# Half rows of the modulation queued behind chosen additions on VectorE in a SwiGLU FFN

## The chip, the cores and the metric

The kernel runs on one core of a Trainium2 chip. The metric is the device time of one execution in microseconds (us), as the median of several runs.

## The reference

Two layers of a diffusion trunk run over 1280 tokens (256 context, 1024 latent) of width 1024, in float32. What matters here is the modulation, computed from the two conditioning vectors, and the FFN that it scales:

```python
def ada_modulation(cond, w, b):
    m = jax.nn.silu(cond) @ w + b
    return jnp.split(m[:, None, :], N_MOD, axis=-1)
...
        sh1, sc1, g1, sh2, sc2, g2 = ada_modulation(cond, w_ada[l], b_ada[l])
...
        h2 = rms_norm(x, norm2_g[l]) * (1.0 + sc2) + sh2
        gate, up = jnp.split(h2 @ w_ffn_in[l], 2, axis=-1)
        x = x + g2 * ((jax.nn.silu(gate) * up) @ w_ffn_out[l])
```

`m` has 6 x 1024 entries per layer and conditioning. The FFN has 2816 hidden features, 22 tiles of 128.

## The kernel before

**Matrix products.** A float32 matrix is split into two parts that TensorE multiplies at full rate: ScalarE casts the high part, VectorE subtracts it (`split`, line 107). Each product is three matmuls (`mm3`, `product`).

**FFN in.** For each of the 22 feature tiles, gate and up are computed for three chunks of tokens: the context (256) and two latent halves (512 each). The two latent halves use a scheme with seven products instead of eight per pair of 512-column blocks: sums of weight quarters are formed on GpSimd (`sums`, lines 156 to 169) and sums of activations once per layer (`act_sums`). A first loop over the features 0 to 6 does their context part and, for the features 1 to 5 (`PRE`), two of the seven products, kept in DRAM. Then `seven(f, ...)` (line 1287) does a whole feature, and `five(f)` (line 1324) the rest of a kept one, with its kept parts loaded (`kept`). The order is 6, then 7, 1, 8, 2, 9, 3, 10, 4, 11, 5, 12, 0, 13 to 21 (`AFTER`). Results go to DRAM (`keep_ft`).

In a seven, a PSUM tile is copied by ScalarE (`copied`) and the accumulation in it goes on; `V.tensor_add(u3, u3, pc)` (L1304) reads the tile `pc`, into which a later product accumulates; `V.tensor_mul(g1, g1, pa_)` (L1308) ends the first latent half, and the additions and multiplications at L1316 and L1318 the second. In a five, `V.tensor_add(u2, p1, pa_)` (L1330) adds the kept product to the first of the PSUM tiles, into which the third product then accumulates; L1334 and L1336 form u3.

**Modulation in the FFN.** A row tile j of the modulation is a dot product of 128 rows of the transposed weight with both conditioning vectors. `ada_half` (line 280) does half of its columns: a load of 128 x 512 into tile `ra` (two buffers), and for each of the two vectors one multiply-reduce on VectorE (L286) with the sum in `mod`; its full output goes to a PSUM tile that nothing reads. The vectors' halves lie in `condh`, one buffer, loaded anew when the half changes. `ada_halves(n)` takes the next n from a list: 16 are issued during the projection before the FFN in each layer, and 48 (layer 0) and 16 (layer 1) at points within `seven` and `five`.

**What sets the order.** TensorE's order is that of the program (`manual_schedule`). The other engines, in this part, are ordered by the tile scheduler, which puts an instruction where it expects it to be ready; each engine and SP's DMA queue then runs its instructions in that order. Weights are fetched ahead (`fetch`, `load_w`) into two `raw` buffers and one more (`rx`), and split into four buffers `w` and three `wh`.

Of the kernel before, what the change touches and what calls it, by code (L numbers as in the profile page):

```python
# [39 lines left out]
FIRST = 7  # L40
# [9 lines left out]
def build(tc, d):  # L50
    nc = tc.nc
    V, S, G, PE = nc.vector, nc.scalar, nc.gpsimd, nc.tensor
# [11 lines left out]
    def nm(s):  # L64
        uid[0] += 1
        return f"{s}_{uid[0]}"
# [138 lines left out]
    def load_w(n, ahead=4):  # L205
        fetch(ahead)
        return [ready.pop(0) for _ in range(n)]
# [72 lines left out]
    def ada_half(l, j, u, pool, first):  # L280
        wt = pool.tile([P, 512], F32, tag="ra", bufs=2, name=nm("ra"))
        nc.sync.dma_start(wt, d["w_adaT"][l, j, :, u * 512:(u + 1) * 512])
        junk = psum()
        for q in range(2):
            o = mods[l][:, j, q:q + 1]
            V.tensor_tensor_reduce(  # L286
                out=junk, in0=wt, in1=pools["condh"][:, q], scale=1.0,
                scalar=cols[:, C_ADA + l * 48 + j:C_ADA + l * 48 + j + 1] if first else o,
                op0=ALU.mult, op1=ALU.add, accum_out=o)
# [252 lines left out]
    for l in range(DEPTH):  # L542
# [420 lines left out]
        for j in range(NQ + 3):  # L963
            if j < NQ:
# [27 lines left out]
                if j > 2 and mix_ld:  # L992
                    c, y = mix_ld.pop(0)
                    t0, n = CH[c]
# [73 lines left out]
        def fpsum(n):  # L1068
            return fps.tile([P, 512], F32, tag="f", bufs=6, name=nm("f"))[:, :n]
# [28 lines left out]
        if l == 0:  # L1098
            late += [(1, j) for j in range(2 * KD)]
        halves = [(a, j, u, x == 0) for b in (early, late) for x, u in enumerate((0, 1) if b is early else (1, 0))  # L1100
                  for a, j in b]

        def ada_halves(n):
            for _ in range(min(n, len(halves))):
                a, j, u, first = halves.pop(0)
                if pools.get("u") != u:
                    pools["u"] = u
                    t = pools["condh"] = fpa.tile([P, 2, 512], F32, tag="ch", name=nm("condh"))
                    nc.sync.dma_start(t, CS[:, u * 512:(u + 1) * 512].partition_broadcast(P))
                ada_half(a, j, u, fpa, first)  # L1110
# [65 lines left out]
        def keep_ft(f, c, sg):  # L1176
            t0, n = CH[c]
            nc.gpsimd.dma_start(FS[l][f, :, t0:t0 + n], sg)  # L1178
# [4 lines left out]
        def copied(ps):  # L1183
            t = fpa.tile([P, 512], F32, tag="cp", bufs=3, name=nm("pc"))
            S.copy(t, ps)
            return t

        def ctx_gate(w):
            pg = fpsum(CH[0][1])
            proj(pg, w, h2[0])  # L1190
            return pg

        def ctx_up(w, f, pg):
            n = CH[0][1]
            pu = fpsum(n)
            if isinstance(w, tuple):
                w = quarter(w[0], 0) + w[1]
            else:
                w = [wslice(w, k) for k in range(KD)]
            mm3(pu, [w[k] + (h2[0][:, 0, k], h2[0][:, 1, k]) for k in range(KD)])  # L1200
            sg = gtile(n)
            S.activation(sg, pg, AF.Silu)
            V.tensor_mul(sg, sg, pu)
            keep_ft(f, 0, sg)
# [21 lines left out]
        def quarter(w, i):  # L1226
            return [wslice(w, 4 * i + j) for j in range(4)]
# [5 lines left out]
        def product(ps, a, b, first=True):  # L1233
            i = 0
            for (wh, wl), (xh, xl) in zip(a, b):
                for y, z in ((wl, xh), (wh, xl), (wh, xh)):
                    PE.matmul(ps, lhsT=y, rhs=z, start=(first and i == 0), stop=(i == 11),  # L1237
                              skip_group_check=not first)
                    i += 1
# [3 lines left out]
        def product1(wg):  # L1243
            ps = fpsum(512)
            product(ps, quarter(wg, 0), b11)
            return wg, ps, copied(ps)


        def product2(wg, p1):
            pb = fpsum(512)  # L1250
            product(pb, quarter(wg, 1), b21)
            g1 = gtile()
            V.tensor_add(g1, p1, pb)
            S.activation(g1, g1, AF.Silu)
            return g1
# [31 lines left out]
        def seven(f, wg, pa_, p1, s24, wh, rest, more, ctx, lead):  # L1287
            first = not callable(rest)
            if lead:
                g1 = product2(wg, p1)  # L1290
            product(pa_, quarter(s24, 0), t2, False)
            u2 = copied(pa_)
            if not lead:
                g1 = product2(wg, p1)
            if ctx:
                pg = ctx_gate(wg)
                ada_halves(int(f > FIRST))
            a21, s31 = (None, rest) if first else rest()
            pc = fpsum(512)
            product(pc, quarter(s31, 1), t1)  # L1300
            product(pa_, quarter(s31, 0), t3, False)
            u3 = copied(pa_)
            nxt = product1(load_w(1, 1)[0]) if more else None
            V.tensor_add(u3, u3, pc)  # L1304
            if ctx and not more:
                ctx_up((a21, wh), f, pg)
            product(pa_, wh, t4, False)
            V.tensor_mul(g1, g1, pa_)  # L1308
            keep_ft(f, 1, g1)
            ada_halves(int(f > FIRST))  # L1310
            if ctx and more:
                ctx_up((a21, wh), f, pg)
            fetch(1)
            product(pc, quarter(s24, 1), b22, False)
            g2 = gtile()
            V.tensor_add(g2, u2, pc)  # L1316
            S.activation(g2, g2, AF.Silu)
            V.tensor_mul(g2, g2, u3)  # L1318
            keep_ft(f, 2, g2)
            ada_halves(int(f != FIRST))  # L1320
            return nxt


        def five(f):
            s24, wh = load_w(1, 1)[0]
            p1, g1 = kept(f, 2, "cp"), kept(f, 1, "g")
            pa_, pc = fpsum(512), fpsum(512)
            product(pa_, quarter(s24, 0), t2)
            u2 = fpa.tile([P, 512], F32, tag="cp", bufs=3, name=nm("pc"))
            V.tensor_add(u2, p1, pa_)  # L1330
            s31 = load_w(1, 1)[0]
            product(pc, quarter(s31, 1), t1)
            u3 = fpa.tile([P, 512], F32, tag="cp", bufs=3, name=nm("pc"))
            V.tensor_add(u3, p1, pc)  # L1334
            product(pa_, quarter(s31, 0), t3, False)
            V.tensor_add(u3, u3, pa_)  # L1336
            ada_halves(int(f > 1))
            product(pc, quarter(s24, 1), b22, False)
            g2 = gtile()
            V.tensor_add(g2, u2, pc)  # L1340
            S.activation(g2, g2, AF.Silu)
            V.tensor_mul(g2, g2, u3)
            keep_ft(f, 2, g2)
            fetch(1)
            product(pa_, quarter(wh, 0), t4, False)
            V.tensor_add(p1, p1, pa_)
            V.tensor_mul(g1, g1, p1)
            keep_ft(f, 1, g1)
# [4 lines left out]
        for f, g in zip(AFTER, AFTER[1:] + (None,)):  # L1353
# [8 lines left out]
            def rest():  # L1362
                return load_w(2, 2)
# [8 lines left out]
        for c in range(3):  # L1372
            t0, n = CH[c]
            xs[c] = opened(xp, f"x{c}", side="right").tile([P, KD, n], F32, name=nm("x"))
        for k in range(KD):
            for c in range(3):
                t0, n = CH[c]
# [198 lines left out]
```

## Time and profile before

| | |
|---|---|
| median of 3 runs | 3073.92 us (3070.77 to 3078.88) |
| the profiled execution | 3073.52 us, span 3071.8 us |
| TensorE busy | 2925.8 us, 95% of the span |
| VectorE busy | 2012.9 us, 66% |
| ScalarE busy | 1109.5 us, 36% |
| GpSimd busy | 682.7 us, 22% |
| mean granted TensorE clock | 0.982 |

The profile is one execution. Busy time is an average over stages with different limits, so the stretch of the FFN is read by itself. Engines are called PE (TensorE), PEld (its weight loads), DVE (VectorE), ACT (ScalarE), POOL (GpSimd) and SP (the queue that issues most loads); L1304 is line 1304 of the kernel before. In a timeline, brackets give the idle time before an instruction and what ended it.

### The profile page before, as it was taken

What the parts mean: (1) busy time and instruction counts of PE and PEld (TensorE: products, weight loads), DVE (VectorE), ACT (ScalarE), POOL (GpSimd) and SP (SyncE); (2) the same over time, 40 slices, a digit from 0 to 9 for tenths busy, and PEclk for the clock granted to TensorE, in tenths of its full rate; (3) what the DMA queues carried; (4) which work ended last, traced back from release to release, by engine and by line L of the source; (5) the groups of instructions that cost most, each with busy time, mean ns of one, the idle gap of its engine ahead of it and who ended that gap; (6) DMA issues with size and microseconds to landing.
All of it is one profiled execution on the core that took longest, in us unless ns stands there. A gap on an engine that the chain in (4) does not pass through costs nothing.

```text
span 3071.8 us, 41522 instructions
## 1 busy us (share of the span) xinstructions
PE 2925.8 (95%) x15800; PEld 2504.0 (82%) x15800; DVE 2012.9 (66%) x3221; ACT 1109.5 (36%) x1887; POOL 682.7 (22%) x756
## 2 busy tenths in 40 slices
PE   7999899998899999999988998999989999999997
PEld 4888788886688888888877887888868888888886
DVE  6767787689864333777677677876874443347777
ACT  4423677163222332211252236761622223222112
POOL 1222200034343333000022222000444433310002
PEclk9999999999999999999999999999999999999998
DMA  6576633444432222512225665434442221152211
GB/s 225 159 219 189 175 93 87 164 139 134 154 117 81 77 73 65 208 72 93 73 97 162 212 177 174 106 96 144 133 139 100 98 76 67 67 188 99 93 62 69
DMA packets 155959, 380.65 MB, mean 124 GB/s; under 512 B 20320, under 2 KB 52336, under 8 KB 155504
## 3 DMA queue, kind: packets, MB, share of 16 engines
q1 hardware_dynamic: 111232, 274.00, 28.3%
q0 software_dynamic: 44240, 103.84, 10.0%
q8 instruction: 124, 2.03, 0.3%
q14 instruction: 75, 0.61, 0.1%
q10 hardware_dynamic: 288, 0.16, 0.0%
HBM read 281.97 MB, written 95.95 MB: 123 GB/s over the span
## 4 chain that ended last, share of the span: by engine, by line
PE 76%; DVE 11%; DMA 5%; issue 4%; ACT 2%; POOL 1%; SPq 0%; DVEq 0%; POOLq 0%; ACTq 0%
PE f L217 32%; PE f L1237 23%; PE pa L217 6%; PE pa L457 4%; PE S L397 4%; PE ps L415 4%; DVE ps L286 2%; DMA kb<-KS 2%; PE ps L932 2%; DVE w L109 1%; DMA ra<-w_adaT 1%; DVE stt L401 1%; ACT E L404 1%; DVE ps L274 1%; DVE E L411 0%
## 5 line engine op out<-in xcount | busy, mean ns | idle before, releaser
L217 PE MATMUL f<-ft,w 128*128 128x512 f32 (+1 forms) x3168 | 614.2, 356 | 0.0
L217 PEld LDWEIGHTS f<-ft,w 128*128 128x128 f32 x3168 | 524.4, 190 | 86.4
L1237 PE MATMUL f<-h,w 128*128 128x512 f32 x2112 | 513.8, 394 | 14.9 <-DVE pc L1304 7.3
L108 ACT CAST w<-raw 128x1024 fp32r<-128x1024 f32 x246 | 254.3, 1049 | 728.1 <-PE f L217 418.9
L109 DVE TENSOR_TENSOR w<-raw,w 128x1024 fp32r<-128x1024 f32 x246 | 306.7, 1255 | 275.4 <-ACT w L108 275.0
L1237 PEld LDWEIGHTS f<-h,w 128*128 128x128 f32 x2112 | 396.4, 190 | 100.4 <-DVE pc L1304 9.1
L1072 DVE SCALAR_TENSOR_TENSOR x<-f,mod,x 128x512 f32<-128x512 f32 (+1 forms) x544 | 341.2, 653 | 168.4 <-PE f L217 164.4
L1237 PE MATMUL f<-T,w 128*128 128x512 f32 x1080 | 274.4, 405 | 26.6 <-DVE pc L1330 14.9
L1237 PEld LDWEIGHTS f<-T,w 128*128 128x128 f32 x1080 | 207.7, 194 | 79.5 <-DVE pc L1330 17.9
L217 PE MATMUL pa<-h,w 128*128 128x512 f32 (+1 forms) x1296 | 249.2, 353 | 0.8 <-DVE vn L635 0.8
L217 PEld LDWEIGHTS pa<-h,w 128*128 128x128 f32 x1296 | 212.2, 192 | 32.3 <-DVE vn L635 1.0
L401 DVE TENSOR_REDUCE stt<-S 128x1 f32<-128x1280 f32 x128 | 189.9, 1487 | 69.3 <-PE S L397 69.3
L457 PE MATMUL pa<-w,h 128*128 128x512 f32 x912 | 220.7, 400 | 11.2 <-DVE w L109 10.6
L316 POOL TENSOR_TENSOR nacc<-nacc,room 128x512 f32<-128x512 f32 (+1 forms) x45 | 51.3, 1140 | 799.1 <-ACT room L315 694.6
L217 PE MATMUL f<-mix,w 128*128 128x512 f32 (+1 forms) x1152 | 225.5, 356 | 0.0
L457 PEld LDWEIGHTS pa<-w,h 128*128 128x128 f32 x912 | 173.7, 193 | 52.1 <-DVE w L109 8.6
L217 PEld LDWEIGHTS f<-mix,w 128*128 128x128 f32 x1152 | 190.8, 190 | 29.5
L397 PE MATMUL S<-kb,aq 128*128 128x512 f32 (+1 forms) x768 | 195.4, 379 | 17.7 <-DMA kb<-KS 10.1
L1178 POOL DMA_DIRECT2D FS<-sg x132 | 73.1, 553 | 532.6 <-DVE sg L1308 244.0
L404 ACT ACTIVATE E<-S,stt 128x1280 f32<-128x1280 f32 x128 | 170.5, 1332 | 39.0 <-DVE stt L401 38.9
L415 PE MATMUL ps<-vt,pt 128*128 128x128 f32 x1280 | 178.5, 280 | 5.3 <-ACT pt L938 5.2
L217 PEld LDWEIGHTS f<-h,w 128*128 128x128 f32 x1392 | 172.7, 192 | 3.9 <-DVE w L109 0.4
(230 smaller groups left out, 3924.8 us busy)
## 6 DMA issues: line engine op xcount, KB each, us to landing
raw<-w_fi SPq DMA_DIRECT2D x112, 512.0 KB, 3.7
ft<-FS SPq DMA_DIRECT2D x44, 640.0 KB, 5.0
ra<-w_adaT SPq DMA_DIRECT2D x96, 256.0 KB, 2.8
FS<-sg POOLq DMA_DIRECT2D x88, 256.0 KB, 2.3
raw<-w_fo SPq DMA_DIRECT2D x44, 512.0 KB, 5.4
kb<-KS SPq DMA_DIRECT2D x64, 320.0 KB, 6.3
raw<-w_adaT SPq DMA_DIRECT2D x32, 512.0 KB, 4.1
raw<-w_in SPq DMA_DIRECT2D x20, 512.0 KB, 3.5
```

What stands on the lines that cost most here:

```text
L108: S.copy(hi, src)
L109: V.tensor_sub(lo, src, hi.bitcast(F32))
L217: PE.matmul(ps, lhsT=a, rhs=b, start=(i == 0), stop=(i == n - 1))
L286: V.tensor_tensor_reduce(out=junk, in0=wt, in1=pools["condh"][:, q], scale=1.0, scalar=cols[:, C_ADA + l * 48 + j:C_ADA + l * 48 + j + 1] ...
L397: PE.matmul(ps[:, o:o + n], lhsT=aq[:, m, q0:q0 + P], rhs=kb[m][1 - p][:, o:o + n], start=(p == 0), stop=(p == 1))
L401: V.reduce_max(st[:, m:m + 1], ps[:, :nkey], axis=AX.X, negate=True)
L404: S.activation(E, ps[:, :nkey], AF.Exp, bias=st[:, m:m + 1], accum_out=st[:, 2 + m:3 + m])
L415: PE.matmul(o[:, :P], lhsT=pt[:, i * P:(i + 1) * P], rhs=vt(b + i), start=(b + i == 0), stop=(b + i == nk - 1))
L457: PE.matmul(ps, lhsT=a[:, y], rhs=wk[:, z], start=(k == 0 and x == 0), stop=(k == KD - 1 and x == 2))
L1072: V.scalar_tensor_tensor(xs[c][:, m], in0=ps, scalar=mods[l][:, g0 + m, COND[c]:COND[c] + 1], in1=xs[c][:, m], op0=ALU.mult, op1=ALU.add)
L1178: nc.gpsimd.dma_start(FS[l][f, :, t0:t0 + n], sg)
L1237: PE.matmul(ps, lhsT=y, rhs=z, start=(first and i == 0), stop=(i == 11), skip_group_check=not first)
```

## The change

A half row is now traced under `tc.issue_after(mark)`, which makes the scheduler place its VectorE instructions behind `mark` on VectorE (an order of issue, no wait for completion). The marks are L1304, L1308 and L1318 in a seven and L1336 in a five. The half that stood behind `ctx_gate` in a seven now stands behind L1304. The conditions on the feature fall away for the first features, so the 48 and 16 halves of the FFN begin with feature 6 (two, then three with feature 7, one with feature 1) and the list is empty earlier: in layer 0 after feature 19, in layer 1 within feature 10.

```diff
+        def ada_after(ins, n):
+            with tc.issue_after(ins.ins):
+                ada_halves(n)
...
             if ctx:
                 pg = ctx_gate(wg)
-                ada_halves(int(f > FIRST))
...
             nxt = product1(load_w(1, 1)[0]) if more else None
-            V.tensor_add(u3, u3, pc)
+            mark = V.tensor_add(u3, u3, pc)
+            if ctx:
+                ada_after(mark, 1)
...
-            V.tensor_mul(g1, g1, pa_)
+            mark = V.tensor_mul(g1, g1, pa_)
             keep_ft(f, 1, g1)
-            ada_halves(int(f > FIRST))
+            ada_after(mark, 1)
...
-            V.tensor_mul(g2, g2, u3)
+            mark = V.tensor_mul(g2, g2, u3)
             keep_ft(f, 2, g2)
-            ada_halves(int(f != FIRST))
+            ada_after(mark, 1)
...
-            V.tensor_add(u3, u3, pa_)
-            ada_halves(int(f > 1))
+            ada_after(V.tensor_add(u3, u3, pa_), 1)
```

TensorE's order is the same in both kernels. The line numbers of the changed kernel are 5 to 6 higher from line 1103 on.

**VectorE where the first loop ends, layer 0.** L286 are the half rows (the multiply-reduce, and the read of its accumulator into `mod`), L1253 evicts a product, L109 splits a weight. Before:

```order
L286 ISA ps_7402,mod_83<-ra_7400,condh_5304,cols 128x512
L286 ISA mod_83 128x1
L286 ISA ps_7402,mod_83<-ra_7400,condh_5304,cols 128x512
L286 ISA mod_83 128x1
L286 ISA ps_7486,mod_83<-ra_7484,condh_5304,cols 128x512
L286 ISA mod_83 128x1
L1253 TENSOR_TENSOR sg_6532<-pc_6516,f_6519 128x512
L109 TENSOR_TENSOR w_6565<-raw_6465,w_6565 128x1024
L286 ISA ps_7486,mod_83<-ra_7484,condh_5304,cols 128x512
L286 ISA mod_83 128x1
L1203 TENSOR_TENSOR sg_6561<-sg_6561,f_6536 128x256
L286 ISA ps_7521,mod_83<-ra_7519,condh_5304,cols 128x512
```

The same evictions and splits in the changed kernel (L1258 is L1253 of before, L1208 is L1203):

```order
L109 TENSOR_TENSOR w_6472<-raw_6470,w_6472 128x1024
L1258 TENSOR_TENSOR sg_6532<-pc_6516,f_6519 128x512
L109 TENSOR_TENSOR w_6565<-raw_6465,w_6565 128x1024
L1208 TENSOR_TENSOR sg_6561<-sg_6561,f_6536 128x256
L109 TENSOR_TENSOR w_6570<-raw_6470,w_6570 128x1024
L109 TENSOR_TENSOR wh_6763<-raw_6761,wh_6763 128x512
L109 TENSOR_TENSOR wh_6827<-raw_6761,wh_6827 128x512
L1208 TENSOR_TENSOR sg_6623<-sg_6623,f_6598 128x256
L1258 TENSOR_TENSOR sg_6655<-pc_6640,f_6642 128x512
```

The half rows between them are gone. The first of them stands behind the multiplication L1308 of feature 6, further on.

**VectorE from feature 9 into the five of feature 3, layer 0.** L1308 and L1318 are the multiplications of the seven, L1330 the first addition of the five. Before:

```order
L1308 TENSOR_TENSOR sg_7358<-sg_7358,f_7319 128x512
L109 TENSOR_TENSOR wh_7704<-raw_7633,wh_7704 128x512
L1316 TENSOR_TENSOR sg_7514<-pc_7373,f_7413 128x512
L109 TENSOR_TENSOR w_7641<-raw_7598,w_7641 128x1024
L1318 TENSOR_TENSOR sg_7514<-sg_7514,pc_7438 128x512
L1330 TENSOR_TENSOR pc_7542<-kt_7524,f_7528 128x512
L1334 TENSOR_TENSOR pc_7561<-kt_7524,f_7529 128x512
```

In the changed kernel (L1314, L1322, L1324, L1336 are L1308, L1316, L1318, L1330 of before):

```order
L1314 TENSOR_TENSOR sg_7383<-sg_7383,f_7344 128x512
L286 ISA ps_7511,mod_84<-ra_7509,condh_5304,cols 128x512
L286 ISA mod_84 128x1
L109 TENSOR_TENSOR wh_7724<-raw_7658,wh_7724 128x512
L286 ISA ps_7511,mod_84<-ra_7509,condh_5304,cols 128x512
L286 ISA mod_84 128x1
L1322 TENSOR_TENSOR sg_7539<-pc_7398,f_7433 128x512
L109 TENSOR_TENSOR w_7666<-raw_7623,w_7666 128x1024
L1324 TENSOR_TENSOR sg_7539<-sg_7539,pc_7458 128x512
L286 ISA ps_7546,mod_84<-ra_7544,condh_5304,cols 128x512
L286 ISA mod_84 128x1
L1336 TENSOR_TENSOR pc_7567<-kt_7549,f_7553 128x512
L286 ISA ps_7546,mod_84<-ra_7544,condh_5304,cols 128x512
```

One whole half row stands between L1308 and L1316, and the first multiply-reduce of the next one ahead of the five's first addition.

**SP's queue where the first loop ends, layer 0.** `raw<-w_fi` are weight loads, `ra<-w_adaT` loads of half rows. Before:

```order
L120 DMA raw_6714<-w_fi 128x1024
L282 DMA ra_7185<-w_adaT 128x512
L282 DMA ra_7220<-w_adaT 128x512
L282 DMA ra_7277<-w_adaT 128x512
L282 DMA ra_7400<-w_adaT 128x512
L282 DMA ra_7484<-w_adaT 128x512
L282 DMA ra_7519<-w_adaT 128x512
L104 DMA raw_6756<-w_fi 128x1024
L282 DMA ra_7576<-w_adaT 128x512
```

In the changed kernel:

```order
L120 DMA raw_6719<-w_fi 128x1024
L104 DMA raw_6761<-w_fi 128x1024
L104 DMA raw_6916<-w_fi 128x1024
L120 DMA raw_6918<-w_fi 128x1024
L104 DMA raw_7025<-w_fi 128x1024
L282 DMA ra_6863<-w_adaT 128x512
L282 DMA ra_6911<-w_adaT 128x512
L104 DMA raw_7060<-w_fi 128x1024
```

The row loads that stood, six in a line, between two weight loads are gone from there; five weight loads now follow each other (the FFN's first two half rows are loaded further ahead).

## Rows read from the trace of the kernel before

**Rows 1.** The profile's page, part 1: busy time of each engine.

```profile
PE 2925.8 (95%) x15800; PEld 2504.0 (82%) x15800; DVE 2012.9 (66%) x3221; ACT 1109.5 (36%) x1887; POOL 682.7 (22%) x756
```

**Rows 2.** Chain of waits in order of time: start us, length us, what.

```profile
772.32 2.96 DMA ra<-w_adaT
...
785.22 4.65 DMA condh<-CS
```

**Rows 3.** Table of stretches, FFN of layer 0: us, busy time (instructions), PEclk, DMA share, GB/s.

```profile
725.00:760.00 35.00, 26.25 (x85) 19.46 (x84) 29.73 (x57) 7.97 (x13) 10.22 (x9) 0.80 0.50 158
...
900.00:1000.00 100.00, 100.00 (x506) 84.69 (x505) 41.25 (x49) 27.07 (x39) 39.58 (x36) 1.00 0.24 82
```

**Rows 4.** Timeline of layer 0, a dense pair: start us, us, engine, line, operation.

```profile
905.15 3.04 PE L217 MATMUL f<-h,w 128*128 128x256 f32 x24
...
908.02 2.91 PE L1237 MATMUL f<-h,w 128*128 128x512 f32 x12
...
944.00 3.04 PE L217 MATMUL f<-h,w 128*128 128x256 f32 x24
```

**Rows 5.** Timeline of TensorE, layer 0's FFN from feature 6 on.

```profile
717.60 2.91 PE L1237 MATMUL f<-h,w 128*128 128x512 f32 x12
...
723.86 4.42 PE L1237 MATMUL f<-h,w 128*128 128x512 f32 x12 [3.35 <-DVE sg L1253]
...
795.15 5.38 PE L1237 MATMUL f<-T,w 128*128 128x512 f32 x12 [6.53 <-DVE pc L1330]
...
845.60 5.49 PE L1237 MATMUL f<-T,w 128*128 128x512 f32 x12 [7.17 <-DVE pc L1330]
...
888.54 3.06 PE L1237 MATMUL f<-T,w 128*128 128x512 f32 x12 [1.22 <-DVE pc L1330]
```

**Rows 6.** The same in layer 1.

```profile
2243.17 2.91 PE L1237 MATMUL f<-h,w 128*128 128x512 f32 x12
...
2268.33 3.07 PE L1237 MATMUL f<-T,w 128*128 128x512 f32 x12 [0.68 <-ACT pc L1185]
...
2309.79 3.04 PE L1237 MATMUL f<-T,w 128*128 128x512 f32 x12
```

**Rows 7.** Half rows' tile: ns min/median/max, first and last start; landing.

```profile
L286 DVE CUSTOM_DVE_ANT_0 ps<-ra,condh,cols x96: 747/758/2995, 553.4 to 2253.2; 128x512 f32<-128x512 f32 x96
...
DMA to landing us min/median/max: 2.4/2.8/6.7
```

**Rows 8.** Timeline of SP's queue, layer 0: start us, us.

```profile
705.54 17.41 SPq L282 DMA_DIRECT2D ra<-w_adaT  x6
...
725.00 0.33 SPq L104 DMA_DIRECT2D raw<-w_fi  x1
```

**Rows 9.** Timeline of layer 0 around a dense five's entry.

```profile
919.44 0.69 DVE L1308 TENSOR_TENSOR sg<-sg,f 128x512 f32<-128x512 f32 x1 [1.95 <-PE f L1237]
...
922.17 0.69 DVE L1316 TENSOR_TENSOR sg<-pc,f 128x512 f32<-128x512 f32 x1 [1.20 <-PE f L1237]
...
924.97 1.77 DVE L1318 TENSOR_TENSOR sg<-sg,pc 128x512 f32<-128x512 f32 x1
...
926.67 0.68 DVE L1330 TENSOR_TENSOR pc<-kt,f 128x512 f32<-128x512 f32 x1
...
927.41 3.04 PE L1237 MATMUL f<-T,w 128*128 128x512 f32 x12
```

**Rows 10.** Timeline of layer 1, entry of its first five.

```profile
2309.78 2.62 PEld L1237 LDWEIGHTS f<-T,w 128*128 128x128 f32 x12 [0.25 <-DVE pc L1330]
```

**Rows 11.** Timeline of VectorE and GpSimd, layer 0: half rows without and with GpSimd's sums.

```profile
754.99 0.75 DVE L286 CUSTOM_DVE_ANT_0 ps<-ra,condh,cols 128x512 f32<-128x512 f32 x1
...
755.66 1.22 DVE L109 TENSOR_TENSOR w<-raw,w 128x1024 fp32r<-128x1024 f32 x1
...
760.44 1.61 POOL L156 TENSOR_TENSOR raw<-raw 128x512 f32<-128x512 f32 x1 [4.51 <-DVE wh L109]
...
760.82 1.79 DVE L286 CUSTOM_DVE_ANT_0 ps<-ra,condh,cols 128x512 f32<-128x512 f32 x1
```

## Prediction, made before the changed kernel ran

> **What bounds the kernel now.** The page's line of busy times comes first: TensorE is busy for 95% of the span, VectorE for 66% [rows 1]. So the time is TensorE's work plus the places where TensorE stands or runs slowly, and a change on VectorE counts only there. The chain of waits shows where such a place is: within the FFN of layer 0 it leaves the matmuls and runs over the load of a half row and that of the two conditioning vectors [rows 2]. The table of stretches fixes the edges. From 900 us on TensorE is busy for 100 of 100 us, at a granted clock of 1.00. From 725 to 760 us it is busy for 26.25 of 35 us, at a granted clock of 0.80 on average (it moves between its two levels of 1.2 and 2.4 GHz), while VectorE is busy for 29.73 of them [rows 3]. The lost time therefore lies in a short stage at the FFN's start, and VectorE is the busiest engine beside it.
>
> TensorE's own rows give the loss. A clean product of 12 matmuls and a context product of 24 are priced from the dense part: between two sevens with a five between them lie 38.85 us, and a context product takes 2.87 us [rows 4]. Such a pair holds 12 products and 2 context products, so a product is (38.85 - 5.74)/12 = 2.76 us. From product1 of the first seven (feature 6) to the third product of the first five lie 16 products and 2 context products, 49.9 us clean. In layer 0 it took 795.15 - 717.60 = 77.55 us; the two pairs after it took 50.45 and 42.94 us [rows 5]. The loss is 27.7 + 11.6 + 4.1 = 43.4 us. In layer 1 the first stretch took 66.62 us, a loss of 16.7 us, and no loss follows [rows 6]. Together that is **60 us**. A part of it is waits with a releaser on VectorE (3.35, 6.53, 7.17 us), a part is products at the lower clock behind them (4.42, 5.38, 5.49 us where 2.9 is usual) [rows 5].
>
> **Why the half rows cause it.** A half row is two multiply-reduces of 747 ns at least (median 758) with a short read of the accumulator each, and a load that lands after 2.8 us [rows 7]. It needs nothing from the FFN, so the scheduler drew it forward: in VectorE's order four and more of them stand between two evictions for which TensorE is waiting. Two `ra` buffers mean that each load also waits for the half two places ahead. SP's queue is in order, so six of these loads held it for 17.4 us, and only at 725.00 us did the next weight load go out [rows 8]. ScalarE, in order too, then had the split of that late weight ahead of copies that TensorE needed. Layer 0 has 48 halves in its FFN and lost 43.4 us; layer 1 has 16 and lost 16.7 us. The line through both is 0.83 us per half and 3.4 us per layer without any.
>
> **The change, part by part.**
> - Removed: all clumps. The order of VectorE shows no half before the second multiplication of feature 6, and SP's shows the next five weight loads ahead of the next half-row load. If nothing else came in, the gain would be 60 us less what is left at a layer's start. Layer 1's row for the copy of a partial sum shows 0.68 us there that hangs on ScalarE alone [rows 6]; the line above says 3.4 us. I take 2 us, between these ends, since the weights of features 6 and 7 now come in time but not with much to spare: 4 us for both layers.
> - Added: the same 64 halves, spread over 20 features of layer 0 and 8 of layer 1 (features 6 and 7 get their full share now, so that the last features have none). In a seven the mark's successors have cover: between the addition into u3 and the product that needs it stand others of 2.76 us each. I cost these halves at nothing; without that cover each would be some 1.5 us.
> - The entry of a five has no cover. VectorE there runs in order: multiplication of g1 at 919.44, eviction of g2 at 922.17 after 1.20 us of idling, multiplication by u3 at 924.97 for 1.77 us, addition of the kept product at 926.67 for 0.68 us; TensorE's third product starts at 927.41, 0.06 us after that ends [rows 9]. In layer 1 the weight load of that product is shown waiting 0.25 us for this addition [rows 10]. The change sets one half between g1 and g2 and the first multiply-reduce of the next ahead of the addition. Seven of the ten fives have that: five in layer 0, the first and third in layer 1; there the second five meets the reload of `condh` and has its half behind the addition.
> - Its price from below: only the last multiply-reduce counts, which takes 0.67 us of the queue between two neighbours [rows 11], so 0.6 us beyond the 0.06. From above: all three meet work on GpSimd. One such multiply-reduce took 1.79 us when GpSimd's sum had begun 0.4 us earlier [rows 11]. Two of these behind g1 bring the eviction of g2 some 2.1 us late, and the third adds 1.7: 3.8 us. I take 1.5 us, nearer the lower end, because GpSimd's sums lie behind when the last one runs and the first two have the 1.20 us of idling to use. Seven of these are 10.5 us (4 to 27).
> - In the Trainium skill, SBUF — State Buffer, "Who interferes with whom" says that a VectorE instruction with two SBUF inputs and a GpSimd instruction reading SBUF exclude each other, the later one standing still for the other's whole length. The trace agrees with the 1.79 us; that rule speaks against putting halves among the weight sums, and by it alone the sum would have 27 us in this place, by the short row 4 us.
> - The `condh` reload, 4.65 us [rows 2], falls between the 24th and 25th half of layer 0's FFN, in a seven whose marks lie further apart than that: nothing. In layer 1 it precedes the ninth, at the second five: 0.5 us.
> - SP and ScalarE: each load of a half now waits for VectorE at a mark, with weight loads behind it. The weights that follow were prepared early in the dense part, and the kept products are loaded ahead of the half rows: nothing.
>
> Sum: 60 - 4 - 10.5 - 0.5 = **45 us** less. The profiled run took 3073.52 us (span 3071.8), 0.4 us under the median of 3073.92, so the forecast is 3029 us against that median. From the bounds, 60 - 1.4 - 4 = 54.6 and 60 - 6.9 - 27 = 26 us of gain, it is 3019 to 3048 us.
>
> **Rivals.**
> 1. *The fives pay the full price.* Each half among GpSimd's sums runs at its slow length, which also pushes those sums and so the split of the weights. For: GpSimd is busy for 39.58 of 100 us there [rows 3]. Against: VectorE has idle time to give in the same stretch (busy 41.25). With 27 us in the fives and 3.4 us a layer the gain is 60 - 7 - 27 = 26: 3048 us.
> 2. *The weights, not the halves, made the loss.* At the first seven the slab splits, three sums on GpSimd and two more splits must fit; if that chain alone held TensorE, the loss would remain, give or take a few us. For: ScalarE's casts stand idle at this place for GpSimd. Against: the loss goes with the number of halves, 43.4 to 16.7. The time would be about 3069 us.
> 3. *VectorE now stands at the mark* (slower). A half whose row has not landed stops the queue; a landing of 2.8 us and two multiply-reduces of 0.76 make 4.3 us. It would happen where SP issues the row only after a raw-weight load that itself waits, once in each of the 28 features. It decides at 60/28 = 2.1 us per feature. At 4.3 it costs 120 against the 60 us: 3134 us. Against: a load is issued one or two halves ahead, and the marks of a dense seven lie 5 us and more apart.
>
> **How the numbers follow.** The forecast has 0.75, rival 1 has 0.15, rivals 2 and 3 have 0.05 each. About 9 us (0.3%) is what a measurement of this kernel can tell from no change. The forecast and rival 1 both lie beyond it: faster 0.90. Rival 2 is same 0.05, rival 3 slower 0.05. The range reaches from 3014 us (all 60 us gained, nothing paid) to 3048 us, the worst of the bounds and rival 1, and leaves out rivals 2 and 3.
>
> **What would show it.** In the changed profile the stretch from product1 of feature 6 to the first five's third product should take about 53 us in both layers instead of 77.6 and 66.6. The granted clock of the FFN's start should be near 1.00. VectorE's waits for half rows and ScalarE's casts waiting for a weight load should be nearly gone from the FFN. TensorE's remaining waits should name the addition of the kept product at a five's entry, of 0.6 to 3.8 us, seven times. Waits on that line near zero would mean the cover was larger than I read; TensorE waiting in the sevens from feature 12 on, or VectorE standing for `ra` there, would mean rival 3; a first seven that still loses over 10 us would mean rival 2.

## The result and the profile after

The changed kernel took 3041.2 us as the median (3037.2 to 3045.7) beside 3072.4 us for the kernel before on the same chip: ratio 0.9895, 95% interval 0.9872 to 0.9919, so 25 to 39 us less. A second series, told below, gave 0.9877 (0.9862 to 0.9892), 33 to 42 us less. Faster was forecast, by 45 us to 3029 us. The range of 3014 to 3048 us holds both medians; the gain was over-rated by 7 to 13 us.

The profile's page first, its line of busy times:

```profile
PE 2917.2 (96%) x15800; PEld 2500.7 (82%) x15800; DVE 1997.3 (66%) x3221; ACT 1110.9 (36%) x1887; POOL 687.8 (23%) x756
```

Then the table of groups by line (busy us, mean ns, idle us before them and what ended it): TensorE's two groups of the FFN that had waits left (L1242 is L1237 of before):

```profile
L1242 PE MATMUL f<-h,w 128*128 128x512 f32 x2112 | 506.9, 391 | 1.1 <-ACT pc L1190 1.1
...
L1242 PE MATMUL f<-T,w 128*128 128x512 f32 x1080 | 265.9, 395 | 19.7 <-DVE pc L1336 16.8 <-ACT pc L1190 2.9
```

TensorE's share of the span hardly moves against [rows 1]. The last column is what to read: of the idle time ahead of the FFN's products, 16.8 us hang on one VectorE line, L1336 (L1330 of before, the addition of the kept product at a five's entry), and 4 us on ScalarE's copy.

The table of stretches, with the start of the FFN (here 722 to 757 us) and the dense part:

```profile
722.00:757.00 35.00, 33.66 (x169) 28.00 (x168) 18.68 (x25) 13.40 (x21) 20.43 (x18) 1.00 0.33 113
...
900.00:1000.00 100.00, 95.96 (x464) 80.03 (x463) 57.14 (x90) 27.77 (x40) 38.06 (x34) 1.00 0.35 116
```

Against [rows 3] the start of the FFN goes from 26.25 to 33.66 us of TensorE work in 35 us, and the granted clock from 0.80 to 1.00. (This execution runs some 7 us later than that of before; from 732.4 to 767.4 us it has 34.33 us of TensorE work, at the same clock.) The dense part, which had no idle time, now loses 4 us in 100. TensorE's timeline says where; layer 0, then layer 1:

```profile
724.49 5.63 PE L1242 MATMUL f<-h,w 128*128 128x512 f32 x24
730.78 3.06 PE L1242 MATMUL f<-T,w 128*128 128x512 f32 x12 [0.67 <-ACT pc L1190]
...
740.03 3.06 PE L1242 MATMUL f<-T,w 128*128 128x512 f32 x12 [0.68 <-ACT pc L1190]
...
778.25 3.07 PE L1242 MATMUL f<-T,w 128*128 128x512 f32 x12 [2.01 <-DVE pc L1336]
...
860.38 4.30 PE L1242 MATMUL f<-T,w 128*128 128x512 f32 x12 [2.02 <-DVE pc L1336]
...
2222.68 5.63 PE L1242 MATMUL f<-h,w 128*128 128x512 f32 x24
...
2276.72 3.07 PE L1242 MATMUL f<-T,w 128*128 128x512 f32 x12 [2.02 <-DVE pc L1336]
...
2317.10 3.07 PE L1242 MATMUL f<-T,w 128*128 128x512 f32 x12 [1.34 <-DVE pc L1336]
```

The stretch that began with waits of 3.35 and 6.53 us [rows 5, 6] takes 778.25 - 724.49 = 53.8 us in layer 0 and 54.0 us in layer 1 (77.6 and 66.6 before). The large waits are gone. In their place every five of layer 0 waits 2.0 us, at 778.25, 819.31, 860.38, 903.02 and 944.07, and four of layer 1 wait 2.02, 1.34, 2.02 and 1.34 us. Behind one of the nine waits, at 860.38, the clock fell once (0.83 on average from 858 to 868 us), and that product and the next took 4.30 and 3.27 us instead of 3.07 and 2.89: 1.6 us.

The time of the FFN's first part, from its first product (L217, `f<-h,w`) to the first row of the down projection (`f<-ft,w`), is the measure of all that follows, since it leaves the rest of the kernel out:

| kernel | layer 0, us | layer 1, us | waits at the fives, us |
|---|---|---|---|
| before | 596.4 | 569.6 | 6.53, 7.17, 1.22 in layer 0, none in layer 1 |
| changed | 566.9 | 562.1 | 2.0 x5; 2.02, 1.34, 2.02, 1.34 |

The gain there is 29.5 + 7.5 = 37.0 us. The spans of the two profiled executions differ by only 27.9 us, because the changed one came to its FFN 7.3 us later and lost 1.8 us between the layers' FFNs, where nothing was changed.

### The profile page after: what moved, and what is told of

It reads as the page before. It is cut to its first block, busy times and chain, and to the rows that moved or that the text cites. A ratio compares the mean times of both kernels' runs of the same rounds, so it can differ in the third digit from the quotient of the medians.

```text
span 3043.9 us, 41519 instructions
## 1 busy us (share of the span) xinstructions
PE 2917.2 (96%) x15800; PEld 2500.7 (82%) x15800; DVE 1997.3 (66%) x3221; ACT 1110.9 (36%) x1887; POOL 687.8 (23%) x756
## 4 chain that ended last, share of the span: by engine, by line
PE 78%; DVE 10%; DMA 4%; issue 3%; ACT 3%; POOL 1%; SPq 0%; DVEq 0%; POOLq 0%; ACTq 0%
PE f L217 33%; PE f L1242 24%; PE pa L217 6%; PE pa L457 4%; PE S L397 4%; PE ps L415 4%; PE ps L932 2%; DMA kb<-KS 2%; DVE w L109 1%; DVE ps L286 1%; DVE stt L401 1%; ACT E L404 1%; DVE ps L274 1%; ACT w L108 1%; DMA raw<-w_adaT 1%
## 5 line engine op out<-in xcount | busy, mean ns | idle before, releaser
L217 PE MATMUL f<-ft,w 128*128 128x512 f32 (+1 forms) x3168 | 615.0, 356 | 0.0
L217 PEld LDWEIGHTS f<-ft,w 128*128 128x128 f32 x3168 | 524.8, 190 | 86.8
L1242 PE MATMUL f<-h,w 128*128 128x512 f32 x2112 | 506.9, 391 | 1.1 <-ACT pc L1190 1.1
L109 DVE TENSOR_TENSOR w<-raw,w 128x1024 fp32r<-128x1024 f32 x246 | 307.6, 1259 | 295.9 <-ACT w L108 295.5
L1242 PEld LDWEIGHTS f<-h,w 128*128 128x128 f32 x2112 | 392.8, 188 | 82.7 <-ACT pc L1190 1.9
L1242 PE MATMUL f<-T,w 128*128 128x512 f32 x1080 | 265.9, 395 | 19.7 <-DVE pc L1336 16.8
L1242 PEld LDWEIGHTS f<-T,w 128*128 128x128 f32 x1080 | 202.4, 188 | 69.9 <-DVE pc L1336 20.8
L217 PE MATMUL pa<-h,w 128*128 128x512 f32 (+1 forms) x1296 | 249.8, 353 | 0.8 <-DVE vn L635 0.8
L217 PEld LDWEIGHTS pa<-h,w 128*128 128x128 f32 x1296 | 212.6, 192 | 32.5 <-DVE vn L635 1.0
L217 PE MATMUL f<-mix,w 128*128 128x512 f32 (+1 forms) x1152 | 225.7, 356 | 0.0
L217 PEld LDWEIGHTS f<-mix,w 128*128 128x128 f32 x1152 | 190.9, 190 | 29.5
L217 PEld LDWEIGHTS f<-h,w 128*128 128x128 f32 x1392 | 172.7, 192 | 3.3
```

The costliest lines, as they stand in the source:

```text
L109: V.tensor_sub(lo, src, hi.bitcast(F32))
L217: PE.matmul(ps, lhsT=a, rhs=b, start=(i == 0), stop=(i == n - 1))
```

## The experiments

**Is the late start of that execution part of the change?** The changed kernel again, unaltered.

> The changed kernel once more, beside the others on one chip. Both theories: ratio to the kernel before 0.987 to 0.992; the FFN stretches 567 and 562 us whatever the whole time is, since the 7 us by which its profile was longer ahead of the FFN is variation between executions; if the change itself had made that, the start of the FFN would again lie near 655 us and not near 648 us.

3036.4 us, ratio 0.9877 (0.9862 to 0.9892). Its FFN began at 649.8 us (before 647.9, first series 655.1) and took 565.7 and 561.8 us, with the same nine waits and no product at the lower clock behind them. So the late start varies from execution to execution, and the waits do not.

**Which halves make the wait?** Theory A is that the halves ahead of the kept product's addition make it late; its rival B, that the weights or the kept product themselves come late. Four kernels take halves out of a seven that a five follows; three of them put these halves behind the five's own mark. With a flag `five_next` (true in a seven that a five follows) the first is

```diff
-        def seven(f, wg, pa_, p1, s24, wh, rest, more, ctx, lead):
+        def seven(f, wg, pa_, p1, s24, wh, rest, more, ctx, lead, five_next=False):
...
             mark = V.tensor_mul(g1, g1, pa_)
             keep_ft(f, 1, g1)
-            ada_after(mark, 1)
+            ada_after(mark, int(not five_next))
...
             mark = V.tensor_mul(g2, g2, u3)
             keep_ft(f, 2, g2)
-            ada_after(mark, 1)
+            ada_after(mark, int(not five_next))
...
-            ada_after(V.tensor_add(u3, u3, pa_), 1)
+            ada_after(V.tensor_add(u3, u3, pa_), 2)
...
```

> In a seven that a five follows, the halves behind the multiplication of g1 and behind that by u3 are gone; the five's mark takes two. Theory A (the chain of VectorE at a five's entry is the limit): TensorE's waits there fall from 2.0 and 1.3 us to 0.3 us or less, the FFN of layer 0 from 567.1 to about 555.5 us, that of layer 1 from 562.2 to about 555.5 us, the whole by 18 us, to about 3023 us. Rival B (the fives wait for their kept product, whose load stands behind half-row loads on SP's queue, or for weights): the waits stay within 0.5 us of 2.0, the whole within 4 us of the changed kernel.

The second moves the half behind g2 alone. The third leaves out the one behind g1's multiplication alone, and the five takes no more than before: the list of halves just runs on to later features. The fourth moves the one behind the addition into u3 (the first mark) alone.

> Only the half behind the multiplication by u3 is moved, into the five behind its mark. Theory A: that half's first multiply-reduce was 0.67 us of the wait at a five's entry, so 2.0 us become 1.3 us; FFN of layer 0 567.1 to about 563 us, of layer 1 562.2 to about 561 us. Rival B: no change of the waits.

> Only the half behind the multiplication of g1 is taken out of the sevens that a five follows (the list runs on to later features). Theory A: 1.34 us of each wait go, so 2.0 become 0.7 us and the waits of 1.3 us in layer 1 nearly vanish; FFN of layer 0 567.1 to about 560 us, of layer 1 562.2 to about 557 us. Rival B: no change of the waits.

> The changed kernel without the half behind the first mark (the addition into u3) in a seven that a five follows; that half goes behind the five's own mark. The other two stay. If the three shares simply add (theory S: 0.34 for the half behind g1's multiplication, 0.67 for the one behind g2's, the rest for this one), the wait at a five with all three falls from 2.0 to 1.0 us. If the first half acts only through pushing GpSimd's sums, and the second pushes them again (theory P), it stays at 1.3 us or more; below 0.7 would mean that this half alone is most of it. One time of 3026 to 3034 us.

TensorE's row at layer 0's first five, in the order both, late3, no2, no1 (one fence per kernel):

```profile
769.24 3.07 PE L1242 MATMUL f<-T,w 128*128 128x512 f32 x12 [1.00 <-DVE pc L1336]
```

```profile
770.37 3.06 PE L1242 MATMUL f<-T,w 128*128 128x512 f32 x12 [1.34 <-DVE pc L1336]
```

```profile
773.09 3.06 PE L1242 MATMUL f<-T,w 128*128 128x512 f32 x12 [1.68 <-DVE pc L1336]
```

```profile
769.04 3.07 PE L1242 MATMUL f<-T,w 128*128 128x512 f32 x12 [1.03 <-DVE pc L1336]
```

The bracket is the wait. With only the first mark's half left it is 1.00 us, where I had counted no such half at all. With that one and g1's it is 1.34, with it and g2's 1.68, with g1's and g2's 1.03. The shares are 1.00, 0.34 and 0.67 and they add to the 2.01 us of the changed kernel: the fourth kernel, expected at 1.0 from the first three, came to 1.03. My expectations for the first (0.3 or less) and third (0.7) were wrong for the same reason, the missed half. The first kernel took 3032.7 us where 3023 was expected, ratio 0.9869 (0.9852 to 0.9885), FFN 561.8 and 560.3 us. The late3 kernel took 562.0 and 560.5 us in the FFN, no2 564.7 and 563.8, no1 561.0 and 559.1 (its single time of 3024.6 us lies just under the 3026 to 3034 expected). Rival B had the waits stay within 0.5 us of 2.0, and they don't; below they fall to 0.34 us with every half and load left in.

**All three out.** The same with none in such a seven and three behind the five's mark.

> The changed kernel, but a seven that a five follows issues no half row at all; the five's own mark (its addition into u3) takes three. If the halves ahead of the five's kept-product addition are the whole of the 2.0 us wait there (theory A, all three of them: the one behind the seven's addition into u3 at about 1.0 us, the one behind g1's multiplication at 0.34, the one behind g2's multiplication at 0.67), TensorE's wait at the fives' third product is 0 to 0.3 us in both layers, as in the dense part of the kernel before; the FFN takes 552 to 556 us per layer from its first product to the first row of the down projection, the whole 3017 to 3025 us. Rival B (the weights or the kept product come late by their own chain, whatever the halves do): the waits stay at 1 us or more and the FFN at 560 us. A further rival C: three halves in a row behind the five's mark make a clump of 4.5 us, which delays the eviction of the five's g2 and shows as a new wait of 1 us or more behind the mark: then FFN 558 us or more.

No wait at any five; FFN 556.0 and 554.5 us; 3019.6 us, ratio **0.9818 (0.9803 to 0.9833)**. Rival C did not show: no wait behind the mark either. A wait of 1.00 us on ScalarE's copy stands in layer 0's last feature, far from any five, behind a cast of the down projection's input on ScalarE.

**What is the floor?** The changed kernel without the FFN's halves.

> The changed kernel with the FFN's 64 half rows of the modulation left out (48 in layer 0, 16 in layer 1; the modulation's tiles are set to zero instead), so neither their loads nor their multiply-reduces run there. It gives the floor of the FFN. Expected: 551 to 554 us per layer in both layers, no wait over 0.3 us at the fives' third product, the small ScalarE waits of 0.5 to 0.7 us at the first seven still there; one time of 3010 to 3022 us. If the FFN still takes 556 us or more with no half in it, part of what I put on the halves belongs to the FFN itself (rival D).

554.8 and 554.3 us (551 to 554 expected), and 3013.7 us in a single run. The three waits on ScalarE's copy at the first seven are there without any half (0.54, 0.74, 0.68 us in layer 0), so they belong to the FFN. Against this floor the kernel before lost 41.6 + 15.2 = 56.8 us to its halves, the changed one 12.1 + 7.8 = 19.9 (18.3 in its second execution, which has no product at the lower clock), the one with all three moved 1.4, of which 1.0 is the wait in the last feature.

**By which way does a half make the addition late?** The timeline of VectorE and GpSimd at layer 0's first five, first in the changed kernel:

```profile
763.06 0.69 DVE L1308 TENSOR_TENSOR pc<-pc,f 128x512 f32<-128x512 f32 x1 [3.53 <-ACT pc L1190]
...
766.15 0.41 DVE L1208 TENSOR_TENSOR sg<-sg,f 128x256 f32<-128x256 f32 x1
766.48 0.68 DVE L109 TENSOR_TENSOR wh<-raw,wh 128x512 fp32r<-128x512 f32 x1
...
766.86 0.56 POOL L1183 DMA_DIRECT2D FS<-sg  x1 [10.39 <-DVE sg L1208]
767.43 1.30 POOL L156 TENSOR_TENSOR raw<-raw 128x512 f32<-128x512 f32 x1
...
770.70 1.62 POOL L158 TENSOR_TENSOR raw<-raw 128x512 f32<-128x512 f32 x1
...
774.23 2.15 POOL L169 TENSOR_TENSOR raw<-raw,raw 128x512 f32<-128x512 f32 x1
...
775.16 1.77 DVE L1324 TENSOR_TENSOR sg<-sg,pc 128x512 f32<-128x512 f32 x1
776.85 0.75 DVE L286 CUSTOM_DVE_ANT_0 ps<-ra,condh,cols 128x512 f32<-128x512 f32 x1
...
777.52 0.68 DVE L1336 TENSOR_TENSOR pc<-kt,f 128x512 f32<-128x512 f32 x1
```

then without any half (there L158, L171, L1325, L1337 and L1243 are L156, L169, L1324, L1336 and L1242, and L111 is the split L109):

```profile
756.77 1.30 POOL L158 TENSOR_TENSOR raw<-raw 128x512 f32<-128x512 f32 x1 [9.42 <-DVE wh L111]
...
763.52 2.16 POOL L171 TENSOR_TENSOR raw<-raw,raw 128x512 f32<-128x512 f32 x1
...
764.45 1.77 DVE L1325 TENSOR_TENSOR sg<-sg,pc 128x512 f32<-128x512 f32 x1
766.14 0.67 DVE L1337 TENSOR_TENSOR pc<-kt,f 128x512 f32<-128x512 f32 x1
...
766.88 3.04 PE L1243 MATMUL f<-T,w 128*128 128x512 f32 x12
```

Even without a half the addition ends at 766.81, 0.07 us ahead of the product that waits for it: the entry has no slack, as [rows 9] showed. And the multiplication by u3 ends some 0.55 us after GpSimd's last sum, in either kernel. Counted from the start of the first mark (L1308 in the changed kernel), in us:

| kernel | first sum starts | last sum ends | multiplication ends | addition starts | third product starts |
|---|---|---|---|---|---|
| before (the five of rows 9) | 2.90 | 11.80 | 12.35 | 12.28 | 13.02 |
| no halves | 2.90 | 11.81 | 12.35 | 12.27 | 13.01 |
| first mark's half only (both) | 4.37 | 12.98 | 13.53 | 13.46 | 14.19 |
| first and g1's (late3) | 4.37 | 13.32 | 13.87 | 13.79 | 14.52 |
| first and g2's (no2) | 4.37 | 12.97 | 13.53 | 14.12 | 14.86 |
| g1's and g2's (no1) | 2.91 | 12.34 | 12.88 | 13.48 | 14.21 |
| all three (changed) | 4.37 | 13.32 | 13.87 | 14.46 | 15.19 |

GpSimd's first sum waits for a split of VectorE (`wh`) and stands, in the changed kernel, behind GpSimd's store of the context's part, which waits for VectorE's multiplication L1208. The half behind the first mark stands ahead of both and holds the first sum back by 1.47 us; the last sum ends 1.17 us later for it. The half behind g1's multiplication runs beside a sum and lengthens it (L158, 1.62 us here against 1.29 with the first mark's half alone). The one behind g2's puts its 0.67 us straight ahead of the addition. The last column grows by 0.16 to 0.18 us more than the waits: in a run of products each starts 2.72 us after the one before and is 2.88 long, and a wait loses that overlap too. What remained was whether the sums act on the multiplication, or whether VectorE's queue is just longer.

The first test keeps every half and moves the multiplication, with the store and half behind it, to behind the addition:

```diff
-            mark = V.tensor_mul(g2, g2, u3)
-            keep_ft(f, 2, g2)
-            ada_after(mark, 1)
+            def close(mark=None):
+                with tc.issue_after(mark.ins) if mark else ExitStack():
+                    mark = V.tensor_mul(g2, g2, u3)
+                keep_ft(f, 2, g2)
+                ada_after(mark, 1)
+            if five_next:
+                todo2.append(close)
+            else:
+                close()
...
-            V.tensor_add(u2, p1, pa_)
+            todo2.pop()(V.tensor_add(u2, p1, pa_))
```

> The changed kernel with all halves where they are in number, but a seven that a five follows does its multiplication of g2 by u3 (with the store of that tile and the half behind it) behind the five's first addition of the kept product, instead of ahead of it. If the addition is late because that multiplication of two SBUF tiles stands still for GpSimd's weight sum and the multiply-reduce runs behind it (theory A2: the halves act by pushing GpSimd's sums into the multiplication), TensorE's wait at the fives' third product goes from 2.0 us to 0 to 0.3, the FFN takes 552 to 557 us per layer, and the whole 3018 to 3026 us, with every half still ahead of the five's mark but one. If instead the eviction and Silu of g2 (or the kept product's load) is what ends late (theory B2), the wait stays at 1.3 us or more.

The same timeline of GpSimd, VectorE and TensorE, where L1327 is the multiplication and L1344 the addition:

```profile
765.61 2.16 POOL L169 TENSOR_TENSOR raw<-raw,raw 128x512 f32<-128x512 f32 x1
...
766.54 0.67 DVE L1344 TENSOR_TENSOR pc<-kt,f 128x512 f32<-128x512 f32 x1
767.14 1.18 DVE L1327 TENSOR_TENSOR sg<-sg,pc 128x512 f32<-128x512 f32 x1
...
767.47 2.95 PE L1242 MATMUL f<-T,w 128*128 128x512 f32 x12
```

The addition (L1344, one input in PSUM) takes 0.67 us while the sum runs beside it. The multiplication behind it (both inputs in SBUF) again ends 0.55 us after the sum. The product goes without a wait, with the halves still behind their marks (one wait of 0.72 us, told below, is left at layer 1's second five): FFN 555.9 and 555.6 us, 3021.5 us, ratio **0.9828 (0.9814 to 0.9841)**. But the queue ahead of the addition is shorter here too, so the second test takes sums away and leaves VectorE's order alone.

> The changed kernel with GpSimd's last two weight sums of each five's own feature left out (20 of them; the weights they make are then other numbers), and the orders on VectorE, ScalarE and SP unchanged row for row, so every half row stands where it did. Theory A2 (the multiplication by u3, two SBUF tiles, stands still for the sum that the halves have pushed beside it: 1.77 us instead of 0.6 to 0.7): the wait at the fives' third product falls from 2.0 us to 0.2 to 0.6. Theory Q (the queue is merely longer by the halves, whatever GpSimd does): it stays at 1.7 to 2.0 us. Whole: 3025 to 3036 us, as one time.

Nothing changed (2.00 to 2.02 us at the fives, 567.2 and 562.2 us): these are the sums of the fives' own weights, which run 20 us later (L168 and L169 at 793.13 and 794.51 us in the changed kernel, where those beside the multiplication start at 772.84 and 774.23). As a control it shows that 20 sums fewer elsewhere are worth nothing. Those beside the multiplication belong to the features 8 to 12:

```diff
-            G.tensor_sub(u[:, :512], u[:, 512:], u[:, :512])
-            G.tensor_sub(u[:, :512], u[:, :512], g[:, :512])
+            if f not in (8, 9, 10, 11, 12):
+                G.tensor_sub(u[:, :512], u[:, 512:], u[:, :512])
+                G.tensor_sub(u[:, :512], u[:, :512], g[:, :512])
```

> The run before took its sums from the wrong features: the trace shows that the two sums beside the multiplication by u3 are those of the next seven's weights (features 8 to 12), the fives' own come 18 us later. Here the last two weight sums of features 8 to 12 are left out instead (20 sums again; those features' weights are then other numbers), with VectorE's, ScalarE's and SP's orders as in the change. Theory A2 (the multiplication stands still for the sum beside it): it takes 0.7 us instead of 1.77, the split ahead of it 1.2 instead of 1.8, and the wait at the fives' third product falls from 2.0 us to 0.2 to 0.6 at all five fives of layer 0. Theory Q (the queue is merely longer by the halves): the wait stays at 1.7 to 2.0 us.

The same timeline, with lines one higher than in the changed kernel (L287 is the half row, L1337 the addition):

```profile
764.68 0.68 DVE L1325 TENSOR_TENSOR sg<-sg,pc 128x512 f32<-128x512 f32 x1
765.28 0.76 DVE L287 CUSTOM_DVE_ANT_0 ps<-ra,condh,cols 128x512 f32<-128x512 f32 x1
...
766.69 3.06 PE L1243 MATMUL f<-T,w 128*128 128x512 f32 x12 [0.34 <-DVE pc L1337]
```

The same queue in the same order, and the multiplication takes 0.68 us instead of 1.77, the wait 0.34 us instead of 2.01, at all five fives of layer 0; FFN 557.0 and 556.7 us. So a longer queue alone would cost 0.34 us. In the changed kernel the halves act through the sums: by the table the first two push the sums' end and with it the multiplication by 1.5 us, and only the last adds its own 0.67.

**What made the loss of before: VectorE's clumps, or SP's queue?** The kernel before with one loaded row that all halves read:

```diff
-        wt = pool.tile([P, 512], F32, tag="ra", bufs=2, name=nm("ra"))
-        nc.sync.dma_start(wt, d["w_adaT"][l, j, :, u * 512:(u + 1) * 512])
+        if "ra" not in pools:
+            wt = pools["ra"] = pool.tile([P, 512], F32, tag="ra", name=nm("ra"))
+            nc.sync.dma_start(wt, d["w_adaT"][l, j, :, u * 512:(u + 1) * 512])
+        wt = pools["ra"]
```

> The kernel before, with the half rows where the scheduler puts them, but with one row of the modulation's weight loaded per use of the pool and read by every half (the other loads are left out, so the modulation's values are of one row). VectorE's multiply-reduces stay in number; SP's queue has no half-row loads to stand behind. Theory T1 (the clumps on VectorE hold TensorE's evictions): the FFN of layer 0 still takes 580 us or more, the whole 3055 to 3075. Theory T2 (the half-row loads hold SP's queue, so weights come late): FFN 553 to 565 us in layer 0, the whole 3015 to 3035. Both in part: between.

SP's and VectorE's timelines, and TensorE's where an addition came late (L288 are the half rows here, L1306 is L1304 of before):

```profile
726.51 3.10 SPq L104 DMA_DIRECT2D raw<-w_fi  x2
...
725.24 1.21 DVE L109 TENSOR_TENSOR w<-raw,w 128x1024 fp32r<-128x1024 f32 x1
...
777.87 0.75 DVE L288 CUSTOM_DVE_ANT_0 ps<-ra,condh,mod 128x512 f32<-128x512 f32 x1
...
781.23 0.75 DVE L288 CUSTOM_DVE_ANT_0 ps<-ra,condh,mod 128x512 f32<-128x512 f32 x1
781.90 0.14 DVE L288 DVE_READ_ACCUMULATOR2_ANT mod<- 128x1 f32 x1
781.90 0.68 DVE L1306 TENSOR_TENSOR pc<-pc,f 128x512 f32<-128x512 f32 x1
...
782.64 3.73 PE L1239 MATMUL f<-h,w 128*128 128x512 f32 x9 [2.65 <-DVE pc L1306]
```

3069.6 us in a single run, FFN 592.9 and 569.0 us (596.4 and 569.6 before). Without half-row loads in SP's queue the next weight load still went out only at 726.51, 0.06 us behind the end of a split on VectorE (L109 at 725.24) that stands in the clump: SP had waited 24.7 us for it. In the kernel before, too, the load at 725.00 [rows 8] came 0.07 us behind such a split. The addition at 781.90 stands behind six multiply-reduces in a row, without any wait for a row of the weight. The clumps on VectorE are nearly the whole loss, the loads about 4 us of it. A clump is also longer than its number of halves says: in the kernel before, five multiply-reduces from 714.14 to 720.94 us took 1.58 to 1.78 us each instead of 0.75, one beside each of five GpSimd sums (1.62 to 1.74 us instead of 1.3). How much of the loss is due to this no run here separates.

**Is it the edge or the new places?** The change with `ada_halves(n)` instead of `with tc.issue_after(ins.ins): ada_halves(n)`.

> The places and numbers of the change, but without the edge that binds a half to its addition: the scheduler may draw each half forward as it did in the kernel before. If the edge is what removes the clumps (theory E), the FFN of layer 0 takes 585 us or more, that of layer 1 565 or more, and the whole 3060 to 3078 us. If the new places and the count per feature do it (theory N), the FFN is as in the change, 567 and 562 us, and the whole 3030 to 3045.

3079.7 us in a single run (3060 to 3078 expected), FFN 595.6 and 569.3 us, with the clumps back:

```profile
800.31 2.92 PE L1241 MATMUL f<-T,w 128*128 128x512 f32 x6 [6.60 <-DVE pc L1335]
```

The new places without the edge keep 1.1 of the 37.0 us. So the edge is needed; the edge at the old places was not run.

**Better than both.** The kernel with the three halves moved (0.9818) and the one with the multiplication moved (0.9828) both lie below the changed one (0.9877, lower end 0.9862), and can't be told apart. Both are within 2.3 us of the floor in the FFN.

## Why the prediction was right, and where its sum failed

- **What the halves cost before.** The prediction read a loss of 60 us from TensorE's rows, 4 of them not to be had. Measured against no halves at all: 56.8. Right.
- **Why.** "Clumps on VectorE" was right. The part on SP ("held it for 17.4 us", [rows 8]) was true as a row and wrong as a cause: with those loads gone the weight load came no sooner, since it waits for a split in VectorE's clump. TensorE's waits on ScalarE's copy stayed too (2.48 and 2.83 us there, 2.71 and 3.12 before).
- **Left at the layers' start, 4 us.** The ScalarE waits are 1.9 and 2.1 us. Right, and they don't come from the halves.
- **"I cost these halves at nothing", for a seven.** This step failed at the seven ahead of a five. The cover was read for the products that follow the mark, 2.76 us each, and there it holds: from feature 12 on no seven waits. But behind the first mark also stand the split and the multiplication (L1208) that release GpSimd's sums, and those sums set when the multiplication two products later ends. That half costs 1.00 us at each five.
- **The fives, 10.5 us in seven places of 1.5 us.** The term was mis-sized: 16.8 us of waits in nine places (2.0 where three halves stand ahead, 1.34 where two do), 1.6 us of lower clock behind one of them, and 9 x 0.16 = 1.4 us of lost overlap, which make the 19.9 us, within its bounds of 4 to 27. The two places not foreseen are the second and fourth fives of layer 1, where the halves behind the first mark and g1 still stand ahead. In part two errors cancelled by luck: the two halves that the term counts, g1's and g2's, cost 1.03 us where 1.5 was taken, and the one it left out costs another 1.00. The value taken rested on "GpSimd's sums lie behind when the last one runs". The last multiply-reduce did run at 0.75 us, but the multiplication ahead of it had waited for those sums, which the earlier halves had pushed. The eviction of g2 did come about 2 us late, as the upper bound had it (9.74 us behind the first mark, 7.78 without halves), but with it as late (9.73) and those two sums gone the wait was 0.34: the eviction did not decide. The Trainium skill's rule on VectorE and GpSimd (SBUF — State Buffer, "Who interferes with whom") was set against this term. The runs agree with it for the multiplication of two SBUF tiles: 1.77 us beside the sum, 0.68 without it, and 0.67 for the addition that reads PSUM.
- **The reload of `condh`, 0.5 us.** VectorE idled 0.18 us for it at the place named, and TensorE not at all; it had waited 1.34 us at that five's entry just before. Where the entry's wait was gone or short, the reload showed at that five: VectorE idled 0.56 us for it with the multiplication moved and 2.26 us with the sums of the features 8 to 12 left out, and TensorE waited 0.72 and 1.34 us for the addition behind it.
- **SP and ScalarE, nothing.** Right: no idle time of VectorE for `ra` is left in the FFN (12.5 us in layer 0 before). The sign named for ScalarE was not met: its casts still wait 18.1 us for weight loads, 28.9 before, where "nearly gone" was forecast.

The sum by the measured terms is 56.8 - 19.9 = 36.9 us where 45 was forecast, and that is what the FFN gained. The whole time by itself does not choose between the forecast and the first rival: 3041.2 us lies 12 us from the one and 7 from the other, and the range held both. Of the rivals, the second fell by the kernel without halves, and with the edge taken out the loss is back. The third did not occur. The first had part of the mechanism, halves that push the sums; but its price was too high, and what costs time is the multiplication that they delay, not the weights.

## What to carry to other kernels

Independent work that a scheduler may place freely can be worth pinning with an edge of order: the same instructions in clumps cost 56.8 us here, pinned 18 to 20, and pinned clear of the one tight place 1.4. Cost such a filler not by its own length but by what stands behind it on its queue and whom that releases: 1.5 us of VectorE cost 1.00, 0.67, 0.34 us or nothing by its place, and the one farthest from the late instruction cost most. Where an addition on the critical path stands behind a multiplication of two SBUF tiles that it doesn't need, try exchanging the two before moving anything else.

## What was unexpected

- The three shares at a five simply add (1.00 + 0.34 + 0.67 = 2.01 us), although two act through GpSimd's sums and one through VectorE's queue.
- A VectorE multiplication of two SBUF tiles ended 0.55 us after GpSimd's sum in every kernel of the table and in the one with the two exchanged, whenever it had begun (1.77 us long, or 1.18 when it began later); an addition with one input in PSUM ran beside the same sum at its usual 0.67 us.
- The same kernel came to its FFN at 655.1 us in one execution and at 649.8 in another. Without the length of the changed stage as a measure, that would have been read as a cost of the change.
